# Lo parts from VectorE throughout, and the first weights of the feed-forward layer split ahead of the activations' sums

## The chip, the cores and the metric

The kernel is one program on one NeuronCore of a Trainium2 chip. The metric is the device time of one execution in microseconds (us); lower is better. Engines are named as in the profile: PE (TensorE's matmuls), PEld (its weight loads), DVE (VectorE), ACT (ScalarE), POOL (GpSimd), SP (SyncE, which here issues DMAs).

## The reference, cut to what matters

One layer of a streaming encoder runs over 1088 tokens: 1024 of a prompt and 64 of a sample, with the same weights.

```
xn = rmsnorm(x);  parts = split(xn @ w_in)             # 1024 x 4120
x = x + concat(ya, yb, yc) @ w_out                     # three mixers: RG-LRU, gated linear attention, SSD
g, buf = causal_dwconv(rmsnorm(x) @ w_gate)            # 1024 x 3072, width 3
x = x + (gelu(g) * (rmsnorm(x) @ w_up)) @ w_down
x = x + sigmoid(rmsnorm(x) @ ple_w_gate) * (p @ ple_w_proj)
y = rmsnorm(x)
```

All data are float32, and the outputs are y and the states of the mixers and convolutions.

## The kernel before, in words

**Three matmuls for one.** A float32 product is made from parts in the format F32R: `hi` is the operand rounded to F32R, `lo` is the operand less `hi`, and `w @ x` becomes `wh @ xh + wh @ xl + wl @ xh` (`mm3`, line 156). Each operand that PE reads, a weight or an activation, is therefore split first, by `split` (line 182): ACT writes `hi` (line 184), then one tensor subtraction writes `lo` (line 188). Which engine subtracts is the point of the change. `split` takes an engine as an argument; without one it alternates between VectorE and GpSimd (`alt`, lines 180 to 188). Weights take `wslots["eng"]`, which is GpSimd at first (line 113). At lines 1079 and 1080, before the last third of the output projection, both are set to VectorE. So up to that line all lo parts of weights and every second one of activations are GpSimd's, and after it none are.

**Tokens and units.** Activations lie with features on partitions, in three chunks of 384, 384 and 320 tokens. Weights come in units of 512 KB: `unit_load` (a DMA of SP into `wr`, two buffers) and `unit_split` (into `wh` and `wl`, three buffers in the pool wpool, others at some places). A unit is used for all chunks before the next. While PE does a unit's matmuls, `tick` lets generators ("lanes") emit the small work of the mixers between them.

**Stages.** By the profile's time: norms and first projections (to about 80 us), the rest of the input projection with the RG-LRU, SSD and attention beside it (to 558), the output projection in three thirds (to 721), the per-layer embedding's projection (to 746), the feed-forward layer's gate and up products (to 1263), its down product, the embedding's gate, and the outputs. At the output projection's entry (line 965, `to_parts`) two large activations per chunk are split: `ya`, which goes to the first third at once, and `qk` (into `qh`, `ql`), which goes to the second third.

**The feed-forward entry.** The gate and up products are made by a scheme of seven block products instead of eight (`quad`, line 1169, 256 output columns at a time, `prod` for one product of 24 matmuls). Its operands are sums and differences of blocks. For the activations they are made once (lines 1115 to 1127), in two pieces of 224 and 320 columns: `t1`, `t2`, `t3`, `b22`, `t4`, each split into hi and lo, and from them the matmuls of all 24 quads are fed. For the weights they are made per quad in `quad_weights` (line 1139): two units are loaded, the first is split as it is (`a11`, `a12`), then the sums `s1`, `s2` (tile s12) and `s3`, `s4` (tile s34) are made by VectorE and split as units, and `a22` is split into `dh`, `dl`. The products come in the order a11 (PSUM qa), s2 with t2 (qb), s1 with t1 (qd), a12 (qa), s3 with t3 (qb), s4 with b22 (qd), a22 with t4 (qb), with evacuations by ACT and VectorE between them.

**Where the tiles lie.** Pools are stacks on two sides of the memory. The tiles of t1 and t2 lie exactly over those of the closed pool xnp, t3, b22 and t4 over the closed pools ept and wx (which the embedding's projection reads), and s12, s34, dh and dl in pool w2 behind them. Pool fp, on the other side, with the gate's buffers `fraw`, lies over the closed pool of the residual X0 and X1, of which the sums are made.

**What sets the order.** Each engine runs its instructions in one fixed order. A planner writes it when the kernel is built: by modelled times, it gives an engine the instruction that stands earliest in the program among those that are ready. An instruction whose data are late can so be passed by later ones, and moving lines in the program changes ranks, not places. SP issues its DMAs in such an order too, and each waits there for its buffer.

Of the kernel before, what the change touches and what calls it, by code (L numbers as in the profile page):

```python
# [9 lines left out]
F32 = mybir.dt.float32  # L10
# [5 lines left out]
PSUM = bass.MemoryType.PSUM  # L16
# [15 lines left out]
HF = 544  # L32
# [3 lines left out]
def f32(ap):  # L36
    return ap.bitcast(F32)
# [3 lines left out]
def trunk(ctx: ExitStack, tc: tile.TileContext, I, O):  # L41
    nc = tc.nc
    V, A, G, PE, SY = nc.vector, nc.scalar, nc.gpsimd, nc.tensor, nc.sync

    const = ctx.enter_context(tc.tile_pool(name="const", bufs=1))
    wpool = ctx.enter_context(tc.tile_pool(name="wpool", bufs=3))
# [5 lines left out]
    smps = [smp]  # L52
# [57 lines left out]
            pass  # L110


    wslots = {"pools": [wpool], "n": 0, "eng": G}

    def unit_load(ap):

# [5 lines left out]
    def unit_split(raw):  # L122

        pool = wslots["pools"][wslots["n"] % len(wslots["pools"])]
        wslots["n"] += 1
        hi = pool.tile(list(raw.shape), F32R, tag="wh", name="wh")
        lo = pool.tile(list(raw.shape), F32R, tag="wl", name="wl")
        split(hi, lo, raw, wslots["eng"])
        return hi, lo

    def unit(ap):
# [45 lines left out]
        hl = [xnq.tile([128, 4, TOK], F32R, tag=n, name=n) for n in ("qh", "ql")]  # L177
        return [tuple(t[:, :, t0:t0 + w] for t in hl) for t0, w in CH]

    alt = [V, G]  # L180

    def split(h, l, x, eng=None):

        A.activation(h, x, AF.Copy)  # L184
        if eng is None:
            eng = alt[0]
            alt.reverse()
        eng.tensor_sub(l, x, f32(h))  # L188

    def feat_terms(u, xs, m, nk, k0=0):  # L190
        hi, lo = u
# [110 lines left out]
    smw = sw.tile([128, KD, 40], F32, name="smw")  # L302
    smh = sw.tile([128, KD, 104], F32R, name="smh")
# [4 lines left out]
    finish(*[lane(xblock(b)) for b in range(3)])  # L308
    wq.append(unit_split(wraw))
    V.tensor_scalar(smh[:, :, 40:64], smw[:, :, 0:24], 0.0, None, op0=OP.mult)  # L310
    split(smh[:, :, 0:40], smh[:, :, 64:104], smw, V)

    def proj(u, c):
        ps = mm_tile()
# [103 lines left out]
    for nm in ("lru_w_r", "lru_w_i"):  # L418
        t = lp.tile([128, 4, 128], F32, name=nm + "_bd")
# [233 lines left out]
    ps = sm_tile()  # L653
    PE.matmul(ps[:, :72], tri, dA.rearrange("p b h -> p (b h)"), start=True, stop=True)
    V.tensor_copy(cum.rearrange("p b h -> p (b h)"), ps[:, :72])
    ps = sm_tile()
# [4 lines left out]
    ps = sm_tile()  # L661
# [44 lines left out]
    for i in range(NS):  # L706
        t = gp.tile([128, 2, 2, 128], F32, name=f"Sg{i}")
# [3 lines left out]
    for i in range(2):  # L711
        t = gp.tile([128, 4, 128], F32, name=f"gsT{i}")
# [227 lines left out]
    xst2 = ExitStack()  # L940
# [6 lines left out]
    XK = [xp.tile([128, 4, TOK], F32, name=f"X{i}") for i in range(2)]  # L947
# [87 lines left out]
    def embedding():  # L1035

        pt8 = ept.tile([128, 8, 256], F32, name="pt8")
        pt1 = ept.tile([64, 256], F32, name="pt1")
        src = tokens("p", 0)
        SY.dma_start(pt8, bass.AP(tensor=src.tensor, offset=src.offset, ap=[[256, 128], [128 * 256, 8], [1, 256]]))  # L1040
        SY.dma_start(pt1, tokens("p", 8))
        yield 12
        for b, (c, off, L) in enumerate(BLK):
            pt = pt8[:, b, :] if b < 8 else pt1
            t0 = CH[c][0] + off
            ps = sm_tile()
            for k in range(2):
                PE.transpose(ps[:, k * 128:k * 128 + L], pt[:L, k * 128:(k + 1) * 128], ident[:L, :L])
            yield 1
            split(pTt[0][:, :, t0:t0 + L], pTt[1][:, :, t0:t0 + L],  # L1050
                  ps.rearrange("p (k t) -> p k t", k=4)[:, 0:2, :L], V)
            yield 1

    lefts = []
# [21 lines left out]
            SY.dma_start(xspill[:, m - 1:m + 1, t0:t0 + w], XK[m // 4][:, m % 4 - 1:m % 4 + 1, t0:t0 + w])  # L1076

    emb = lane(embedding())
    alt[:] = [V]
    wslots["eng"] = V  # L1080
    wslots["pools"], wslots["n"] = [wpool, wpool, wpool, wx], 0
    normed = []
    add_proj(WO[1024:1536], ys["c"], 4, lambda c: normed.append(lane(norm_rows(c))), spill)
# [4 lines left out]
    for q in range(2):  # L1088
        u = unit(I["ple_w_proj"][0][:, 512 * q:512 * q + 512])
        for m in range(4):  # L1090
            for c, (t0, w) in enumerate(CH):
                ps = mm_tile()
# [18 lines left out]
    t1, t2 = [half(n, rp1) for n in ("t1", "t2")]  # L1111
    rp2 = rst.enter_context(tc.tile_pool(name="rp2", bufs=1, reuse_waits="tile"))
    t3, b22, t4 = [half(n, rp2) for n in ("t3", "b22", "t4")]
    w2 = rst.enter_context(tc.tile_pool(name="w2", bufs=1, reuse_waits="tile"))
    for a, n in ((0, 224), (224, 320)):
        s = slice(a, a + n)
        x11, x12 = XK[0][:, :, a:a + n], XK[0][:, :, HF + a:HF + a + n]
        x21, x22 = XK[1][:, :, a:a + n], XK[1][:, :, HF + a:HF + a + n]
        V.tensor_sub(x12, x12, x11)
        split(t1[0][:, :, s], t1[1][:, :, s], x12)  # L1120
        V.tensor_sub(x12, x22, x12)
        split(t2[0][:, :, s], t2[1][:, :, s], x12)
        V.tensor_sub(x11, x12, x11)
        V.tensor_sub(x21, x21, x12)
        split(t3[0][:, :, s], t3[1][:, :, s], x11)
        split(b22[0][:, :, s], b22[1][:, :, s], x22)
        split(t4[0][:, :, s], t4[1][:, :, s], x21)
    b11, b21 = [tuple(t[:, 4 * i:4 * i + 4, :] for t in lefts) for i in range(2)]
    xst2.close()

    fst, qpst = ExitStack(), ExitStack()
    fp = fst.enter_context(tc.tile_pool(name="fp", bufs=1, side="right", reuse_waits="tile"))
    qp = qpst.enter_context(tc.tile_pool(name="qp", bufs=1, space=PSUM, reuse_waits="tile"))
    smps[0] = qpst.enter_context(tc.tile_pool(name="smq", bufs=2, space=PSUM, reuse_waits="tile"))
    fouts = fp.tile([128, 96], F32, name="fouts")
    WG, WU, WD = I["ffn_w_gate"][0], I["ffn_w_up"][0], I["ffn_w_down"][0]
    wslots["pools"] = [wpool]

    def quad_weights(ap):

        raw0, raw1 = unit_load(ap[:, 0:128]), unit_load(ap[:, 128:256])
        a11, a12, a21, a22 = raw0[:, 0:4, :], raw0[:, 4:8, :], raw1[:, 0:4, :], raw1[:, 4:8, :]
        al = unit_split(raw0)
        s12 = w2.tile([128, 8, 128], F32, tag="s12", name="s12")
        s1, s2 = s12[:, 0:4, :], s12[:, 4:8, :]
        V.tensor_add(s1, a21, a22)
        V.tensor_sub(s2, s1, a11)
        be = unit_split(s12)
        s34 = w2.tile([128, 8, 128], F32, tag="s34", name="s34")
        s3, s4 = s34[:, 0:4, :], s34[:, 4:8, :]  # L1150
        V.tensor_sub(s3, a11, a21)
        V.tensor_sub(s4, a12, s2)
        ga = unit_split(s34)
        de = tuple(w2.tile([128, 4, 128], F32R, tag=n, name=n) for n in ("dh", "dl"))
        split(de[0], de[1], a22)
        part = lambda u, i: tuple(t[:, 4 * i:4 * i + 4, :] for t in u)
        return {"a11": part(al, 0), "a12": part(al, 1), "s1": part(be, 0), "s2": part(be, 1), "s3": part(ga, 0),
                "s4": part(ga, 1), "a22": de}

    def prod(ps, w, x, new):  # L1160
        for i in range(2):
            n = 0
            for k in range(4):
                for wt, xt in ((w[0], x[0]), (w[0], x[1]), (w[1], x[0])):
                    PE.matmul(ps[:, i, :HI], wt[:, k, :], xt[:, k, HI * i:HI * i + HI], start=new and n == 0,  # L1165
                              stop=n == 11, skip_group_check=True)
                    n += 1

    def quad(ap, take11, o12, o21, o22):

        w = quad_weights(ap)
        A_, B_, D_ = [qp.tile([128, 2, 512], F32, tag=n, name=n) for n in ("qa", "qb", "qd")]
        pa, pb, pd = [t[:, :, :HI] for t in (A_, B_, D_)]
        o12, o21, o22 = [t.rearrange("p (i n) -> p i n", i=2) for t in (o12, o21, o22)]
        prod(A_, w["a11"], b11, True)
        A.activation(o21, pa, AF.Copy)  # L1176
        prod(B_, w["s2"], t2, True)
        V.tensor_add(o12, o21, pb)
        prod(D_, w["s1"], t1, True)
        V.tensor_add(o22, o21, pd)  # L1180
        prod(A_, w["a12"], b21, False)
        take11(pa)
        prod(B_, w["s3"], t3, False)
        V.tensor_add(o22, o22, pb)
        prod(D_, w["s4"], b22, False)
        V.tensor_add(o12, o12, pd)
        prod(B_, w["a22"], t4, False)
        V.tensor_add(o21, o21, pb)
# [21 lines left out]
    Lh, Rh = slice(0, HF), slice(HF, TOK)  # L1210
    for p in range(FF // 256):
        cols = slice(256 * p, 256 * p + 256)
        raws = []
        for i in range(2):
            r = fp.tile([128, 2 + TOK], F32, tag="fraw", name="fraw", bufs=2)
            G.memset(r[:, 0:2], 0.0)
            raws.append(r)
        g0, g1 = [r[:, 2:] for r in raws]

        def to_g11(ps):  # L1220
            A.activation(g0[:, Lh].rearrange("p (i n) -> p i n", i=2), ps, AF.Copy)

        quad(WG[:, cols], to_g11, g0[:, Rh], g1[:, Lh], g1[:, Rh])
        ts = [conv_rows(2 * p + i, raws[i]) for i in range(2)]
        u0 = fp.tile([128, HF], F32, tag="u0", name="u0")
        u1 = fp.tile([128, TOK], F32, tag="u1", name="u1")

        def to_u11(ps):
            t = ts[0][:, Lh].rearrange("p (i n) -> p i n", i=2)
            V.tensor_mul(t, t, ps)  # L1230

        quad(WU[:, cols], to_u11, u0, u1[:, Lh], u1[:, Rh])
        V.tensor_mul(ts[0][:, Rh], ts[0][:, Rh], u0)
        V.tensor_mul(ts[1], ts[1], u1)
        for i in range(2):
            SY.dma_start(hidd[:, 2 * p + i, :], ts[i])

    ps = sm_tile()
# [166 lines left out]
```

## Time and profile before

| | |
|---|---|
| time, median of 3 runs | 1673.28 us (1671.46 to 1674.77) |
| the profiled execution's own time | 1674.28 us |
| its span | 1672.6 us |
| PE busy | 1611.8 us, 96% of the span |
| DVE, ACT, POOL busy | 1064.8, 701.7, 205.7 us |
| mean granted clock of TensorE | 0.982 |

The profile is of one execution. Busy time is the time in which an engine has an instruction under way; for PE, whose matmuls overlap, a window that is fully busy has no gap. The clock is the share of the full 2.4 GHz that was granted: matmuls of a stretch at the lower level of 1.2 GHz take about twice their time. In the lists in order of time a row has its start and length in us, the engine and line, what it writes and reads, its shape, and in brackets how long the engine stood idle before it and which instruction ended that. A line can be a helper's: all lo parts are line 188, all hi parts line 184.

### The profile page before, as it was taken

To read this page: it belongs to the slowest core of one execution; us is meant where nothing else is said; L and a number is where in the kernel's file an instruction comes from. 1 tells how busy PE (TensorE), PEld (TensorE's weight loads), DVE (VectorE), ACT (ScalarE), POOL (GpSimd) and SP (SyncE) were. 2 spreads that over 40 slices of the span, in tenths; PEclk is the share of its full clock that TensorE was granted. 3 is DMA by queue.
4 is the path that set the end of the run, shared out by engine and by line. 5 is a ranking of instruction groups with operands and counts; after the bars stand their busy time and mean duration, and the time that the engine had idled before them with its cause. 6 is when DMAs were issued, how large, how long until landed. Compare 5 with 4: busy or idle time off the path is not lost.

```text
span 1672.6 us, 27037 instructions
## 1 busy us (share of the span) xinstructions
PE 1611.8 (96%) x10990; PEld 1556.1 (93%) x10990; DVE 1064.8 (64%) x1824; ACT 701.7 (42%) x1041; POOL 205.7 (12%) x330
## 2 busy tenths in 40 slices
PE   6999999999999799988999999999999999999997
PEld 6898889878999799988999999999998999999996
DVE  5588883786554853797666766666665544436834
ACT  5578863585722411363333333333333221203526
POOL 3322232221221420000000000000000000000000
PEclk8999999999999999998999999999999999999998
DMA  8332123112652311332222222222228533110223
GB/s 229 89 82 56 48 57 88 39 26 76 174 166 84 98 40 51 114 142 61 78 78 66 88 74 77 75 77 77 77 78 310 175 92 104 55 51 14 79 61 124
DMA packets 169112, 151.80 MB, mean 91 GB/s; under 512 B 11218, under 2 KB 157532, under 8 KB 168988
## 3 DMA queue, kind: packets, MB, share of 16 engines
q1 hardware_dynamic: 159628, 145.62, 28.4%
q10 hardware_dynamic: 9360, 4.46, 0.9%
q8 instruction: 86, 1.41, 0.3%
q14 instruction: 38, 0.31, 0.1%
HBM read 111.26 MB, written 38.79 MB: 90 GB/s over the span
## 4 chain that ended last, share of the span: by engine, by line
PE 61%; DVE 3%; ACT 1%; issue 0%; DVEq 0%; ACTq 0%
PE mm L163 30%; PE qb L1165 13%; PE qd L1165 9%; PE qa L1165 8%; DVE nr_t L218 0%; PE sm L1327 0%; DVE ql L188 0%; ACT yo L1328 0%; DVE X L1062 0%; DVE l L188 0%; DVE yc L986 0%; DVE dl L188 0%; PE sm L216 0%; ACT yo L1338 0%; DVE X L992 0%
## 5 line engine op out<-in xcount | busy, mean ns | idle before, releaser
L163 PE MATMUL mm<-dh,wh 128*128 128x384 f32 (+1 forms) x768 | 252.1, 329 | 2.7 <-ACT wh L184 2.5
L163 PE MATMUL mm<-dl,wh 128*128 128x384 f32 (+1 forms) x768 | 252.0, 328 | 0.8 <-DVE dl L188 0.8
L184 ACT ACTIVATE wh<-wr 128x1024 fp32r<-128x1024 f32 x102 | 107.7, 1058 | 344.7 <-PE mm L163 233.5
L163 PE MATMUL mm<-dh,wl 128*128 128x384 f32 (+1 forms) x768 | 251.4, 328 | 0.0
L163 PE MATMUL mm<-h,wh 128*128 128x384 f32 (+1 forms) x528 | 178.4, 339 | 12.9 <-ACT h L184 8.5
L163 PE MATMUL mm<-l,wh 128*128 128x384 f32 (+1 forms) x528 | 176.9, 335 | 6.2 <-DVE l L188 6.2
L163 PE MATMUL mm<-h,wl 128*128 128x384 f32 (+1 forms) x528 | 179.6, 340 | 0.0
L163 PEld LDWEIGHTS mm<-dh,wh 128*128 128x128 f32 x768 | 145.2, 189 | 3.5 <-ACT wh L184 2.8
L992 DVE TENSOR_TENSOR Xq<-Xq,mm 128x384 f32<-128x384 f32 (+1 forms) x144 | 76.0, 530 | 113.6 <-PE mm L163 113.0
L163 PEld LDWEIGHTS mm<-dl,wh 128*128 128x128 f32 x768 | 145.1, 189 | 1.7 <-DVE dl L188 1.6
L163 PEld LDWEIGHTS mm<-dh,wl 128*128 128x128 f32 x768 | 144.8, 189 | 0.5 <-DVE wl L188 0.3
L163 PE MATMUL mm<-ql,wh 128*128 128x384 f32 (+1 forms) x432 | 143.9, 333 | 0.2 <-POOL ql L188 0.2
L163 PE MATMUL mm<-qh,wh 128*128 128x384 f32 (+1 forms) x432 | 141.9, 328 | 0.0
L163 PE MATMUL mm<-qh,wl 128*128 128x384 f32 (+1 forms) x432 | 141.4, 327 | 0.0
L163 PEld LDWEIGHTS mm<-h,wh 128*128 128x128 f32 x528 | 100.7, 191 | 18.3 <-ACT h L184 9.4
L188 POOL TENSOR_TENSOR wl<-wr,wh 128x1024 fp32r<-128x1024 f32 x40 | 95.8, 2397 | 170.1 <-ACT wh L184 162.6
L184 ACT ACTIVATE wh<-s 128x1024 fp32r<-128x1024 f32 x48 | 51.0, 1061 | 155.2 <-PE qd L1165 55.0
L1165 PE MATMUL qa<-qh,wh 128*128 128x272 f32 x384 | 110.9, 289 | 0.6 <-ACT fraw L1176 0.6
L1165 PE MATMUL qa<-ql,wh 128*128 128x272 f32 x384 | 110.8, 288 | 0.0
L1165 PE MATMUL qa<-qh,wl 128*128 128x272 f32 x384 | 110.4, 288 | 0.0
L163 PEld LDWEIGHTS mm<-l,wh 128*128 128x128 f32 x528 | 101.1, 191 | 9.4 <-DVE l L188 7.0
L163 PEld LDWEIGHTS mm<-h,wl 128*128 128x128 f32 x528 | 101.1, 191 | 2.5 <-issue 0.6
(397 smaller groups left out, 4182.0 us busy)
## 6 DMA issues: line engine op xcount, KB each, us to landing
wr<-in_w_in_dram SPq DMA_DIRECT2D x32, 512.0 KB
hidd<-ft SPq DMA_DIRECT2D x24, 544.0 KB
wr<-in_ffn_w_gate_dram SPq DMA_DIRECT2D x24, 512.0 KB
wr<-in_ffn_w_up_dram SPq DMA_DIRECT2D x24, 512.0 KB
wr<-in_ffn_w_down_dram SPq DMA_DIRECT2D x24, 512.0 KB
st<-hidd SPq DMA_DIRECT2D x12, 768.0 KB
wr<-in_w_out_dram SPq DMA_DIRECT2D x12, 512.0 KB
s_cb<-cumd SPq DMA_DIRECT2D x18, 256.0 KB
```

The costliest lines, as they stand in the source:

```text
L163: PE.matmul(out, w, x, start=(k == 0), stop=(k == n - 1))
L184: A.activation(h, x, AF.Copy)
L188: eng.tensor_sub(l, x, f32(h))
L992: V.tensor_add(xv(c, m), xv(c, m), ps[:, :w])
L1165: PE.matmul(ps[:, i, :HI], wt[:, k, :], xt[:, k, HI * i:HI * i + HI], start=new and n == 0, stop=n == 11, skip_group_check=True)
```

## The change

All lo parts are VectorE's from the beginning: `alt`, the engine argument of `split` and `wslots["eng"]` go, and with them the two lines that switched engines on the way. And `quad_weights` is called for the first 256 columns of the gate ahead of the activations' sums instead of behind them; `quad` takes finished weights. For this the definitions of the weights stand ahead of the sums, and the pools fp, qp and smq are opened after them as before. The other 23 calls of `quad_weights` stand where they stood.

```diff
-    wslots = {"pools": [wpool], "n": 0, "eng": G}
+    wslots = {"pools": [wpool], "n": 0}
...
-        split(hi, lo, raw, wslots["eng"])
+        split(hi, lo, raw)
...
-    alt = [V, G]
-
-    def split(h, l, x, eng=None):
+    def split(h, l, x):
 
         A.activation(h, x, AF.Copy)
-        if eng is None:
-            eng = alt[0]
-            alt.reverse()
-        eng.tensor_sub(l, x, f32(h))
+        V.tensor_sub(l, x, f32(h))
...
-    alt[:] = [V]
-    wslots["eng"] = V
...
-    for a, n in ((0, 224), (224, 320)):
...
-    b11, b21 = [tuple(t[:, 4 * i:4 * i + 4, :] for t in lefts) for i in range(2)]
-    xst2.close()
...
     WG, WU, WD = I["ffn_w_gate"][0], I["ffn_w_up"][0], I["ffn_w_down"][0]
     wslots["pools"] = [wpool]
...
+    first = quad_weights(WG[:, 0:256])
+    for a, n in ((0, 224), (224, 320)):
+        s = slice(a, a + n)
+        x11, x12 = XK[0][:, :, a:a + n], XK[0][:, :, HF + a:HF + a + n]
+        x21, x22 = XK[1][:, :, a:a + n], XK[1][:, :, HF + a:HF + a + n]
+        V.tensor_sub(x12, x12, x11)
+        split(t1[0][:, :, s], t1[1][:, :, s], x12)
+        V.tensor_sub(x12, x22, x12)
+        split(t2[0][:, :, s], t2[1][:, :, s], x12)
+        V.tensor_sub(x11, x12, x11)
+        V.tensor_sub(x21, x21, x12)
+        split(t3[0][:, :, s], t3[1][:, :, s], x11)
+        split(b22[0][:, :, s], b22[1][:, :, s], x22)
+        split(t4[0][:, :, s], t4[1][:, :, s], x21)
+    b11, b21 = [tuple(t[:, 4 * i:4 * i + 4, :] for t in lefts) for i in range(2)]
+    xst2.close()
...
-    def quad(ap, take11, o12, o21, o22):
-
-        w = quad_weights(ap)
+    def quad(w, take11, o12, o21, o22):
+
...
-        quad(WG[:, cols], to_g11, g0[:, Rh], g1[:, Lh], g1[:, Rh])
+        quad(quad_weights(WG[:, cols]) if p else first, to_g11, g0[:, Rh], g1[:, Lh], g1[:, Rh])
...
-        quad(WU[:, cols], to_u11, u0, u1[:, Lh], u1[:, Rh])
+        quad(quad_weights(WU[:, cols]), to_u11, u0, u1[:, Lh], u1[:, Rh])
```

## Rows read from the trace of the kernel before

**Rows 1.** The page's part 1: busy us and share of the span, instructions, of each engine.

```profile
PE 1611.8 (96%) x10990; PEld 1556.1 (93%) x10990; DVE 1064.8 (64%) x1824; ACT 701.7 (42%) x1041; POOL 205.7 (12%) x330
```

**Rows 2.** Windows: us, then busy (x instructions) of PE, PEld, DVE, ACT, POOL; clock, DMA share, GB/s.

```profile
80.00:260.00 180.00, 173.41 (x1092) 159.74 (x1092) 147.56 (x313) 138.47 (x237) 60.20 (x97) 0.98 0.25 64
260.00:420.00 160.00, 157.56 (x1199) 133.72 (x1198) 103.77 (x253) 94.58 (x155) 31.06 (x51) 1.00 0.21 57
...
558.00:594.00 36.00, 26.53 (x134) 24.94 (x133) 34.46 (x31) 11.35 (x14) 15.64 (x5) 0.86 0.25 79
...
746.00:780.00 34.00, 26.52 (x177) 25.58 (x177) 25.39 (x28) 15.21 (x18) 2.84 (x10) 0.80 0.21 63
```

**Rows 3.** PE in order of time, feed-forward's entry: start, us, instruction [idle before <-releaser].

```profile
745.77 0.31 PE L163 MATMUL mm<-pTh,wl 128*128 128x320 f32 x1
...
749.16 0.29 PE L1165 MATMUL qa<-qh,wl 128*128 128x272 f32 x1
...
754.12 0.59 PE L1165 MATMUL qb<-t2h,wh 128*128 128x272 f32 x1 [4.68 <-ACT wh L184]
...
759.17 0.59 PE L1165 MATMUL qb<-t2h,wl 128*128 128x272 f32 x1 [2.17 <-DVE wl L188]
```

**Rows 4.** The chain that ended last: start, us, what; the second quad's first product.

```profile
779.25 3.01 PE qa L1165 x24
```

**Rows 5.** ACT in order of time, feed-forward's entry.

```profile
748.70 0.94 ACT L184 ACTIVATE t4h<-X 128x896 fp32r<-128x896 f32 x1
...
753.02 1.04 ACT L184 ACTIVATE wh<-s 128x1024 fp32r<-128x1024 f32 x1
```

**Rows 6.** DVE in order of time, feed-forward's entry.

```profile
745.48 1.48 DVE L188 TENSOR_TENSOR t2l<-X,t2h 128x1280 fp32r<-128x1280 f32 x1
...
748.28 0.69 DVE L1146 TENSOR_TENSOR s<-wr 128x512 f32<-128x512 f32 x1
...
753.70 1.48 DVE L188 TENSOR_TENSOR t3l<-X,t3h 128x1280 fp32r<-128x1280 f32 x1
...
757.90 1.21 DVE L188 TENSOR_TENSOR wl<-s,wh 128x1024 fp32r<-128x1024 f32 x1
```

**Rows 7.** PE in order of time, output projection's entry.

```profile
574.28 0.63 PE L163 MATMUL mm<-l,wh 128*128 128x320 f32 x1 [5.66 <-DVE l L188]
...
584.22 0.69 PE L163 MATMUL mm<-h,wh 128*128 128x384 f32 x1 [2.29 <-DVE X L992]
```

**Rows 8.** DVE in order of time: operations with two SBUF inputs, three stretches.

```profile
146.21 2.29 DVE L450 SCALAR_TENSOR_TENSOR l_xc<-lraw,cols,l_xc 128x384 f32<-128x384 f32 x1 [0.39 <-ACT l_xc L448]
...
538.95 0.56 DVE L899 SCALAR_TENSOR_TENSOR yc<-yc,gth 128x384 f32<-128x384 f32 x1
...
559.91 2.76 DVE L209 TENSOR_TENSOR nr_t<-nr_t,gy 128x384 f32<-128x384 f32 x1
...
570.05 4.18 DVE L188 TENSOR_TENSOR l<-ya,h 128x1280 fp32r<-128x1280 f32 x1
```

**Rows 9.** POOL in order of time: lo parts beside those.

```profile
145.66 2.42 POOL L188 TENSOR_TENSOR wl<-wr,wh 128x1024 fp32r<-128x1024 f32 x1 [0.57 <-ACT wh L184]
...
562.20 10.68 POOL L188 TENSOR_TENSOR ql<-qk,qh 128x1536 fp32r<-128x1536 f32 x3
```

**Rows 10.** PE in order of time: two waits for DVE.

```profile
150.13 1.16 PE L479 MATMUL sm<-l_xc,lru_w_r_bd 128*128 128x384 f32 x2 [2.14 <-DVE l_xc L450]
...
718.33 0.42 PE L163 MATMUL mm<-h,wh 128*128 128x320 f32 x1 [2.08 <-DVE X L992]
```

**Rows 11.** Line 188 on POOL: ns min/median/max, first and last start us, forms.

```profile
L188 POOL TENSOR_TENSOR wl<-wr,wh x40: 2352/2394/2607, 12.7 to 632.4; 128x1024 fp32r<-128x1024 f32 x40
```

**Rows 12.** PE in order of time: the first projection matmul.

```profile
20.47 1.01 PE L163 MATMUL mm<-h,wh 128*128 128x384 f32 x2 [4.91 <-ACT h L184]
```

**Rows 13.** Waits, whole span: engine line <- releaser: us in total, times, longest us.

```profile
POOL wl L188 <- ACT wh L184: 162.6, 35, 14.1
...
DVE wl L188 <- ACT wh L184: 53.5, 75, 2.8
```

More of the change, by code (lines that the diff above doesn't have):

```diff
@@ L310, in trunk @@
     V.tensor_scalar(smh[:, :, 40:64], smw[:, :, 0:24], 0.0, None, op0=OP.mult)
-    split(smh[:, :, 0:40], smh[:, :, 64:104], smw, V)
+    split(smh[:, :, 0:40], smh[:, :, 64:104], smw)
     def proj(u, c):
@@ L1050, in embedding @@
             split(pTt[0][:, :, t0:t0 + L], pTt[1][:, :, t0:t0 + L],
-                  ps.rearrange("p (k t) -> p k t", k=4)[:, 0:2, :L], V)
+                  ps.rearrange("p (k t) -> p k t", k=4)[:, 0:2, :L])
             yield 1
@@ L1114, in trunk @@
     w2 = rst.enter_context(tc.tile_pool(name="w2", bufs=1, reuse_waits="tile"))
-    for a, n in ((0, 224), (224, 320)):
[L1116 to L1127, printed above, removed]
-    b11, b21 = [tuple(t[:, 4 * i:4 * i + 4, :] for t in lefts) for i in range(2)]
-    xst2.close()
[L1131 to L1135, printed above, removed]
     WG, WU, WD = I["ffn_w_gate"][0], I["ffn_w_up"][0], I["ffn_w_down"][0]
@@ L1158, in quad_weights @@
                 "s4": part(ga, 1), "a22": de}
+    first = quad_weights(WG[:, 0:256])
[14 more added lines that the diff above has]
+    xst2.close()
+    fst, qpst = ExitStack(), ExitStack()
+    fp = fst.enter_context(tc.tile_pool(name="fp", bufs=1, side="right", reuse_waits="tile"))
+    qp = qpst.enter_context(tc.tile_pool(name="qp", bufs=1, space=PSUM, reuse_waits="tile"))
+    smps[0] = qpst.enter_context(tc.tile_pool(name="smq", bufs=2, space=PSUM, reuse_waits="tile"))
+    fouts = fp.tile([128, 96], F32, name="fouts")
     def prod(ps, w, x, new):
```

## The prediction

> **What bounds the kernel now.** I read the busy line of the page first: PE is busy 1611.8 us of a span of 1672.6 [rows 1], so 60.8 us are idle. The reader is to see that no other engine comes near: time can only come from PE's idle time, or from matmuls that run at the lower clock. The windows by stage came next [rows 2]: PE is short by 9.5 us in 558 to 594 (clock 0.86), by 7.5 us in 746 to 780 (clock 0.80) and by 6.6 us in 80 to 260 (clock 0.98). These three stretches hold nearly all that this change can touch. Then I read, for each, PE's order of time and the orders of DVE, ACT and POOL beside it, to see which instruction ended each wait.
>
> *The feed-forward entry.* The first product (qa) ends at 749.3. The second (qb) has to wait 4.68 us for `wh` from ACT, issues two matmuls, does a few of later products, and waits 2.17 us more for `wl` from DVE [rows 3]. The matmul after the wait takes 0.59 us where the last one before it took 0.29: the clock has fallen to its lower level, 1.2 GHz, and the mean over the window is 0.80. The second quad starts at 779.25 [rows 4]. A product of 24 matmuls takes 3.01 us at the full clock [rows 4], so without any wait the six left would end at 749.3 + 6 x 3.01 = 767.4. The entry costs 11.9 us.
>
> Why is `wh` late? ACT makes it at 753.02, behind the six hi parts of t3, b22 and t4, the third of which starts at 748.70 [rows 5]; DVE makes `wl` at 757.90, behind all their lo parts [rows 6]. The order is the program's: the sums and splits stand ahead of the weights. It isn't that the weights could come much sooner: `s12` lies in w2, whose first bytes lie over the end of the closed pool wx (by the tile sizes: t3, b22 and t4 take 52,224 bytes of the 57,344 of ept and wx, then comes `s12`, over the lo part of the projection's second unit). So its first write must wait for the last projection matmul, which starts at 745.77 [rows 3]; the 0.69 us addition stands at 748.28, right behind DVE's older work [rows 6].
>
> *The output projection's entry.* PE waits 5.66 us for a lo part of DVE and later 2.29 us for an accumulation of DVE [rows 7]. DVE is busy 34.46 of these 36 us [rows 2], but not with work: four operations with two SBUF inputs, the first a 2.76 us one at 559.91 and the last one of 4.18 us at 570.05 [rows 8], stand beside POOL's lo parts, 10.68 us for three [rows 9]. The same kind and size takes 0.56 us at 538.95 [rows 8]; a 1280-column lo part takes 1.48 us [rows 6]. Each ends about its own duration after a POOL operation ends (572.88 + 1.4 = 574.2): DVE was held until POOL had finished. The four lost 2.2 + 2.4 + 2.6 + 2.7 = 9.9 us.
>
> **The change, part by part.** Durations are from one execution: 1674.28 us, a span of 1672.6 and 1.7 around it. It lies 1.0 above the median of the runs.
>
> *1. Weights ahead of the sums.* No instruction is added; seven loads, sums and splits change their rank. The two loads are issued as early as before (their buffers are free long ahead), and SP has nothing behind them that waits; the `fp` and quad PSUM pools open later in the text, at the same places. What moves is the order on ACT and DVE after 746. DVE is free at 746.9, behind t2's lo part [rows 6]. s1 and s2 take 0.6 us each from start to start (0.69 with their ends): 748.1. ACT has then three pieces of 0.85 us (dh, t3, b22) behind it and is free at 748.7, where it started t4 before [rows 5]: `wh` is there at 749.7. DVE meanwhile does s3, s4 and the 1.4 us sum that stood ahead of s1 before, to 750.7, then `wl` 1.15 us: 751.9. PE has issued two matmuls of qb by then, 142 of the six products are left, at 3.01 / 24 = 0.125 us: 769.7. That is 9.5 us sooner than 779.25. Bounds: with `wl` straight behind `wh` 10.8, with no wait at all 11.9; if the order stays, nothing. The two waits of together 2.5 us lie near the 2.08 us after which the clock kept its level at 718.33, and near the 2.14 us after which it fell at 150.13 [rows 10]; a fall costs 1.5 us by estimate, a dozen matmuls at twice their time. I take **-9.5**, from 0 to -11.9.
>
> What is late next: t3. Its lo parts stand behind the weights now: 751.9 + 0.6 (dl) + 1.4 and, at the same rate, 1.0 (t3's two parts, [rows 6]) + 1.15 (`wl` of s34) = 756.0, where the last t3 part ended at 755.2 before. It also frees X0, over which the gate's buffer lies, so ACT's evacuation of qa comes at 756.6 and the fourth product can start at 757.2; PE asks for it at 757.7. b22 is done near 759 (asked for at 763.7) and t4 near 762 (at 766.7). These fit, with 0.5 us of slack at the first and 4 us at the others.
>
> *2. The lo parts move to DVE.* 40 weight units at 2.39 us on POOL [rows 11] become 1.15 us each on DVE, 46 us; eight activation parts of 512 columns and one of 256, three of `qk` and one of `yc` add 6 + 5 + 2: 59 us in all, over the first 640 us. Against that stand the times for which POOL held DVE.
>
> At 558 to 594: two units, 2.3, and the three `qk` parts 1.7 + 1.7 + 1.4: 7.1 us more, 9.9 less. From 559.91 to 574.23, the end of the lo part for which PE waited, DVE's 14.3 us become 14.3 - 9.9 + 4.8 + 1.15 = 10.3: the part ends 4.0 us sooner. The second unit may stand in the way of the accumulation for which PE waits 2.29 us: 1.15 back. I take **-3.5**; ends: -8.8 if the `qk` parts, wanted only one projection later, go behind; +2 if both units and all three stand ahead and the release is half of what I read.
>
> At 80 to 260: three times PE waits for `l_xc` of DVE, one of them 2.14 us at 150.13 [rows 10]. Each time the first operation of `l_xc` takes 2.29 us, held by a POOL lo part that began 0.55 us before it [rows 8, 9]. With `wl` ahead of it on DVE it would end at 145.6 + 1.15 + 0.56 = 147.3 and not 148.5, 1.2 us sooner. The other nine of the twelve units there bring 1.15 us each and are hardly paid back. DVE has 32 us idle in the stretch [rows 2]. I take 1 us per wait, **-3**, from -8 (the waits, 5.8, and the clock behind two of them) to the loss of the last rival. From 260 to 420 PE is short by only 2.4 us, and DVE has 56 us idle for 8 us of added units [rows 2]: nothing, plus or minus 2; the ten units up to 558 go the same way.
>
> At the start: PE's first projection matmul waits 4.91 us for the third block's hi part [rows 12], behind DVE's scalings. Ahead of them come now one unit (1.15) and two activation parts (0.6 each), 2.4 in all, less what POOL no longer holds up there. **+1**, from 0 to +2.5.
>
> *The wait that is added.* A lo part waits for ACT's hi part. POOL stood in this wait for 162.6 us, 35 times, harming nobody; where DVE does it, it stands 0.71 us each time (53.5 us, 75 times) [rows 13], with convolutions and accumulations queued behind it. Where ACT is early, as in the forecast, that is idle time that DVE has.
>
> The Trainium skill bears on this in Perfetto Trace Analysis, section Optimizing Scalar/DVE Operations: with a saturated DVE, handing work to GpSimd may pay, though the two share a port and a trade between them might not help. Its first half speaks against this change, its second half is what the held operations show; by the first half alone the output projection's entry would lose, by the time of the first rival.
>
> **The sum.** -9.5 - 3.5 - 3 + 1 = -15.0: 1674.3 becomes 1659.3 for such an execution, and 1658.3 from the median; between the two I say 1659.
>
> **Rivals.**
> - *DVE stays the bound at 558 to 594.* If nothing is given back, 34.46 + 7.1 = 41.6 us of DVE in a stretch of 36: 5.6 us later, not 3.5 sooner, so -5.9: 1668. For it: the 96% load. Against it: the four held operations. Chance 0.08.
> - *The change doesn't do what it says at the feed-forward.* `s12` can't be written before 746, and a planner orders each engine by when an operation is ready: by then t3's parts are ready too and may keep their place. Then only -5.5: 1668.5. Against it: dh, of still lower rank, went ahead of t3 before. Chance 0.08.
> - *The gain is handed back inside the first pair.* If t3 slips by 4 us behind the weights, PE waits at the fourth product, at the lower clock: 1665. Chance 0.12.
> - *DVE gains more*: `qk` parts go behind, the `l_xc` waits vanish with their clock falls: -9.5 - 8 - 7: 1649. Chance 0.10.
> - *Slower: the lo parts clog DVE's queue.* In 80 to 420 DVE holds 19 units, each 1.15 us of work and 0.71 us of wait for ACT ahead of convolutions that PE wants. If all twelve of 80 to 260 come through to PE: 12 x 1.86 = 22.3, with the other terms (-12) +10: 1684. It decides from the seventh that comes through. For it: 147.56 of 180 us busy. Against it: 32 us idle, and weights made a unit ahead. Chance 0.08.
>
> **Chances and range.** Forecast 0.54, within 1653 to 1666. A measurement of this kernel can tell about 0.2%, 3.3 us, from no change. Faster by more: the forecast, the third and fourth rival and half of the first two, 0.84; within it: the other half, 0.08; slower: 0.08. The range, 1650 to 1670, leaves out the slower rival and about half of the 1649 one.
>
> **What would show it.** Right: qb's `wh` on ACT before 750.5 (in time from the end of the projection), the second quad 20 to 22 us after qa's end instead of 30; POOL without lo parts and the 558 to 594 window with no two-input operation of 384 columns on DVE above 0.7 us; `l_xc` waits under 1.5 us. Wrong: ACT or DVE with t3 ahead of `s12`; a wait at the fourth product; PE short in 80 to 420 by more than the 9 us of now.

## The result, and the profile after

The changed kernel takes 1654.82 us (median of 4, 1652.04 to 1658.90) against 1672.37 before: a ratio of 0.9899, with a 95% interval of 0.9870 to 0.9927. Timed a second time beside the experiments below it took 1651.37 us (1650.81 to 1651.61) against 1673.04: 0.9875 (0.9857 to 0.9893). The forecast was 1659, from 1650 to 1670, with a narrower band of 1653 to 1666 for it: the first timing lies in that band, the second 1.6 us under it. Direction and range held. The terms of the sum missed on both sides, and in part made up for one another.

The profiled execution took 1654.01 us. The page's part 1, which answers to [rows 1]:

```profile
PE 1605.0 (97%) x10990; PEld 1551.4 (94%) x10990; DVE 1074.0 (65%) x1877; ACT 699.8 (42%) x1040; POOL 84.1 (5%) x277
```

POOL has lost 122 us, and DVE has gained 9, although 59 us of lo parts moved to it. By that estimate some 50 us of DVE's busy time before were no work of its own.

The windows, as in [rows 2], the third and fourth moved to where the same work now lies:

```profile
80.00:260.00 180.00, 177.46 (x1151) 164.89 (x1150) 151.30 (x330) 139.00 (x240) 34.49 (x86) 1.00 0.27 72
260.00:420.00 160.00, 159.35 (x1204) 135.15 (x1202) 108.92 (x267) 101.08 (x160) 16.40 (x44) 1.00 0.21 55
551.60:587.60 36.00, 33.23 (x183) 31.60 (x182) 31.45 (x42) 11.07 (x13) 0.00 (x0) 0.95 0.29 93
731.60:765.60 34.00, 30.27 (x224) 29.55 (x224) 31.04 (x37) 18.97 (x22) 3.56 (x13) 0.95 0.27 79
```

PE's idle time fell in every one, and the clock rose in the first, third and fourth. Following the same matmul through both traces gives each term (the forecast's stretches end a little elsewhere):

| up to | before | after | forecast of this stretch | measured |
|---|---|---|---|---|
| first projection matmul | 20.47 | 24.24 | +1 | +3.8 |
| first matmul of the values' projection | 214.24 | 210.42 | -3 | -7.6 |
| statistics at the output projection's entry | 557.88 | 551.49 | 0 | -2.6 |
| embedding's projection | 721.46 | 706.94 | -3.5 | -8.1 |
| first feed-forward product | 746.15 | 731.74 | 0 | +0.1 |
| second quad (chain of waits) | 779.25 | 758.89 | -9.5 | -6.0 |
| end of the span | 1672.6 | 1652.3 | 0 | +0.1 |

A second profile of the changed kernel, from its second timing, gives each of these within 0.7 us, except the last, which is -1.5 there.

The feed-forward entry in PE's order of time (a row has its start and length, and in brackets the wait and what ended it), answering to [rows 3]; under it two pieces of the chain of waits, answering to [rows 4]:

```profile
735.50 0.39 PE L1160 MATMUL qb<-t2h,wh 128*128 128x272 f32 x1 [0.47 <-ACT wh L182]
...
736.76 0.39 PE L1160 MATMUL qb<-t2h,wl 128*128 128x272 f32 x1 [0.49 <-DVE wl L183]
...
745.24 0.59 PE L1160 MATMUL qa<-qh,wh 128*128 128x272 f32 x1 [2.69 <-ACT fraw L1170]
```

```profile
757.89 1.00 PE qb L1160 x8
758.89 1.13 PE qa L1160 x9
```

The two waits that the reordering was to shorten fell from 4.68 and 2.17 us to 0.47 and 0.49. In their place stands one of 2.69 us at the fourth product, for ACT's evacuation of qa. The matmul behind it takes 0.59 us: the clock is at its lower level again.

The output projection's entry on PE, answering to [rows 7], and DVE beside it, answering to [rows 8]:

```profile
561.21 0.78 PE L211 MATMUL sm<-nr_t,ones 128*128 128x320 f32 x2 [0.67 <-DVE nr_t L204]
...
564.09 0.61 PE L163 MATMUL mm<-h,wh 128*128 128x320 f32 x1 [2.10 <-DVE X L987]
```

```profile
552.04 0.55 DVE L204 TENSOR_TENSOR nr_t<-nr_t,gy 128x384 f32<-128x384 f32 x1
552.51 1.22 DVE L183 TENSOR_TENSOR wl<-wr,wh 128x1024 fp32r<-128x1024 f32 x1
553.64 3.42 DVE L183 TENSOR_TENSOR ql<-qk,qh 128x1536 fp32r<-128x1536 f32 x2
...
557.38 1.48 DVE L183 TENSOR_TENSOR ql<-qk,qh 128x1280 fp32r<-128x1280 f32 x1
...
559.18 1.48 DVE L183 TENSOR_TENSOR l<-ya,h 128x1280 fp32r<-128x1280 f32 x1
560.59 0.48 DVE L204 TENSOR_TENSOR nr_t<-nr_t,gy 128x320 f32<-128x320 f32 x1
...
563.45 0.49 DVE L987 TENSOR_TENSOR X<-X,mm 128x384 f32<-128x384 f32 x1
```

The 0.55 us operation took 2.76 us before and the lo part of ya 4.18. Three ql parts and a unit now stand ahead of that lo part, and PE doesn't wait for it. The 320-column nr_t operation and the accumulations into X come behind it; before, that nr_t operation and two accumulations stood ahead (at 567.03, 562.59 and 566.35).

The waits for l_xc, answering to [rows 10]:

```profile
124.05 0.91 PE L474 MATMUL sm<-l_xc,lru_w_r_bd 128*128 128x384 f32 x2 [1.40 <-DVE l_xc L445]
...
152.87 0.91 PE L474 MATMUL sm<-l_xc,lru_w_r_bd 128*128 128x384 f32 x2 [0.27 <-DVE l_xc L445]
...
181.50 0.91 PE L474 MATMUL sm<-l_xc,lru_w_r_bd 128*128 128x384 f32 x2 [0.82 <-DVE l_xc L445]
```

### The profile page after: what moved, and what is told of

Same layout as the page of the kernel before. It is cut to its first block, busy times and chain, and to the rows that moved or that the text cites. A ratio compares the mean times of both kernels' runs of the same rounds, so it can differ in the third digit from the quotient of the medians.

```text
span 1652.3 us, 26989 instructions
## 1 busy us (share of the span) xinstructions
PE 1605.0 (97%) x10990; PEld 1551.4 (94%) x10990; DVE 1074.0 (65%) x1877; ACT 699.8 (42%) x1040; POOL 84.1 (5%) x277
## 4 chain that ended last, share of the span: by engine, by line
PE 87%; DVE 6%; ACT 3%; DMA 2%; issue 1%; SPq 0%; ACTq 0%; POOL 0%; DVEq 0%; POOLq 0%
PE mm L163 49%; PE qb L1160 13%; PE qd L1160 9%; PE qa L1160 9%; DMA xsp<-x 1%; PE po L794 1%; DMA wr<-in_w_in_dram 1%; PE sm L579 1%; PE sm L800 1%; PE po L787 1%; PE sm L581 0%; PE sm L575 0%; DVE l_xc L445 0%; PE sm L474 0%; DVE xs L445 0%
## 5 line engine op out<-in xcount | busy, mean ns | idle before, releaser
L183 DVE TENSOR_TENSOR wl<-wr,wh 128x1024 fp32r<-128x1024 f32 x102 | 124.8, 1225 | 63.3 <-ACT wh L182 63.1
```

The source lines that it names most:

```text
L183: V.tensor_sub(l, x, f32(h))
```

## The experiments

Theory: the two parts act at different places; GpSimd's subtractions hold VectorE's operations with two SBUF inputs, and the first part's gain is the end of that; the second part's gain is cut by the evacuation of qa. Rivals: the gain is one of VectorE's order or load; the fourth product's wait is a late VectorE's. Times below are medians, and ratios stand against the kernel before on the same chip, which took 1672.5, 1673.0 and 1672.1 us in the three sets of runs. Each set had a chip of its own, and the changed kernel was timed again only in the second; where a run of another set is compared with it, the ratios count.

**Each part alone.** The first without the second:

```diff
-    first = quad_weights(WG[:, 0:256])
...
-        quad(quad_weights(WG[:, cols]) if p else first, ...)
+        quad(quad_weights(WG[:, cols]), ...)
```

> Only the first part of the change: all lo parts are VectorE's, the first pair's weights stay behind the sums. Theory (the two parts are separate, and the first one brings what the changed kernel had gained by the start of the feed-forward layer, 14.4 us): the first feed-forward product starts near 731.7, the second quad 29 to 31 us behind the end of qa as before, time 1659 to 1661. Rival (the terms as I sized them, -5.5 in all): 1667 to 1669.

1658.01 us, ratio 0.9908 (0.9896 to 0.9921): 14.5 sooner, 1 us better than the theory had it. The first product starts at 730.31, the second quad 29.3 us behind the end of qa, and the wait for `wh` is back:

```profile
738.28 0.58 PE L1159 MATMUL qb<-t2h,wh 128*128 128x272 f32 x1 [4.70 <-ACT wh L182]
```

The second without the first (`alt`, `eng` and both switches as before, `first` ahead of the sums):

> Only the second part: the first pair's weights ahead of the sums, the lo parts on their engines of before. Theory: nothing moves before 746; the second quad starts 24 us behind the end of qa and not 30, with a wait of 2 to 3 us at the fourth product, time 1667 to 1669 for an execution of 1674. Rival (the fourth product's wait comes from VectorE being late by work of the first part): no such wait, second quad 20.5 us behind, 1664 to 1665.

1666.65 us, 0.9954 (0.9939 to 0.9970): 5.9 sooner, which lies between theory and rival. The trace decides: the fourth product waits the same 2.69 us with the lo parts on their old engines, so the rival falls. The second quad starts 22.4 us behind the end of qa and not 24, as the clock stayed up behind that wait:

```profile
760.88 0.39 PE L1167 MATMUL qa<-qh,wh 128*128 128x272 f32 x1 [2.69 <-ACT fraw L1177]
```

The two add up to 20.4; the whole change brought 17.6 and 21.7 in its two timings.

**What the fourth product waits for.** From the first product's start to the third quad's, two quads without a wait take 14 x 3.01 = 42.1 us. Before it was 54.0, in the changed kernel 48.0 and 48.2, with the first part alone 53.7. With t3 ahead:

```diff
     for a, n in ((0, 224), (224, 320)):
...
         split(t3[0][:, :, s], t3[1][:, :, s], x11)
+    for a, n in ((0, 224), (224, 320)):
...
         split(b22[0][:, :, s], b22[1][:, :, s], x22)
         split(t4[0][:, :, s], t4[1][:, :, s], x21)
```

> The changed kernel with the sums of both column pieces up to t3 ahead of the splits of b22 and t4, so that X0 is read for the last time two VectorE operations (2.0 us) sooner. Theory A (X0's last read holds the gate's buffer, and so the evacuation of qa): the wait of 2.69 us at the fourth product falls to 0.7 and the clock stays up, 3 to 4 us sooner than the changed kernel, 1651. Rival B (ScalarE's own queue of hi parts holds that evacuation, at best till 743.4 where it was 744.58): the wait falls by 1.2 us only, 1 to 1.5 us sooner, 1653.5.

1650.72 us, 0.9866 (0.9852 to 0.9880). In the changed kernel DVE's last t3 part and ACT's rows ahead of the evacuation are these:

```profile
738.76 1.09 DVE L183 TENSOR_TENSOR b22l<-X,b22h 128x896 fp32r<-128x896 f32 x1
739.76 1.09 DVE L183 TENSOR_TENSOR t4l<-X,t4h 128x896 fp32r<-128x896 f32 x1
740.76 1.48 DVE L1142 TENSOR_TENSOR X<-X,X 128x1280 f32<-128x1280 f32 x1
742.16 1.48 DVE L183 TENSOR_TENSOR t3l<-X,t3h 128x1280 fp32r<-128x1280 f32 x1
```

```profile
742.46 1.06 ACT L182 ACTIVATE wh<-wr 128x1024 fp32r<-128x1024 f32 x1 [1.21 <-PE qd L1160]
743.42 1.25 ACT L182 ACTIVATE t4h<-X 128x1280 fp32r<-128x1280 f32 x1
744.58 0.60 ACT L1170 ACTIVATE fraw<-qa 128x544 f32<-128x544 f32 x1
```

X0 is free at 743.64, and ACT is in t4's hi part until 744.58. With t3 ahead, PE's two waits and ACT's evacuation:

```profile
740.41 0.39 PE L1163 MATMUL qa<-qh,wh 128*128 128x272 f32 x1 [1.58 <-ACT fraw L1173]
...
744.56 0.39 PE L1163 MATMUL qb<-t3h,wh 128*128 128x272 f32 x1 [0.86 <-DVE fraw L1175]
```

```profile
737.84 1.08 DVE L183 TENSOR_TENSOR b22l<-X,b22h 128x896 fp32r<-128x896 f32 x1
```

```profile
737.43 1.25 ACT L182 ACTIVATE t4h<-X 128x1280 fp32r<-128x1280 f32 x1
738.79 1.06 ACT L182 ACTIVATE wh<-wr 128x1024 fp32r<-128x1024 f32 x1
739.75 0.60 ACT L1173 ACTIVATE fraw<-qa 128x544 f32<-128x544 f32 x1
```

X0 is free at 737.9, when DVE starts b22, but ACT evacuates at 739.75, behind its own hi parts. The wait fell by 1.11 us, as rival B had it, and a new one of 0.86 came behind it. (The total is nearer theory A, but it can't tell the two: the changed kernel's own ratios are 0.9899 and 0.9875.) The two-quad stretch is 46.7 us, the 1.3 less being nearly all clock: with the second part alone, where the 2.69 us wait stayed and the clock didn't fall, it is 46.7 too. So for this order both X0's last read and ACT's queue hold the evacuation. The other way is to take X0 out of it:

```diff
+    fp2 = fst.enter_context(tc.tile_pool(name="fp2", bufs=1, side="right", reuse_waits="tile"))
     fouts = fp.tile([128, 96], F32, name="fouts")
+    fp.tile([128, 2624], F32, name="pad")
...
-            r = fp.tile([128, 2 + TOK], F32, tag="fraw", name="fraw", bufs=2)
+            r = (fp, fp2)[i].tile([128, 2 + TOK], F32, tag="fraw", name="fraw")
```

> The changed kernel with the gate's buffer that takes the evacuation of qa laid behind X0 and X1 in memory, not over X0; the rest of the buffers lie over X0 and X1 in another order. Theory A (the overlap with X0 causes the fourth product's wait): ScalarE evacuates qa near 741.5, no wait of over 0.5 us at the fourth product, its first 13 matmuls at full clock: 2.7 + 1.6 = 4.3 us sooner than the changed kernel, 1650.5. Rival B (ScalarE's queue is late anyway): less than 1.5 us sooner, 1653.5. Rival C: the buffers that lie over X0 and X1 now make another wait, no sooner than the changed kernel.

1650.51 us, 0.9864 (0.9851 to 0.9877). ACT now has the evacuation between b22 and t4, and the wait at the fourth product is gone; two short ones follow:

```profile
742.79 0.60 ACT L1172 ACTIVATE fraw<-qa 128x544 f32<-128x544 f32 x1
```

```profile
747.91 0.39 PE L1162 MATMUL qa<-qh,wh 128*128 128x272 f32 x1 [0.71 <-ACT fraw L1217]
...
748.79 0.39 PE L1162 MATMUL qd<-b22h,wh 128*128 128x272 f32 x1 [0.49 <-DVE fraw L1176]
```

The two-quad stretch is 45.5 us, 2.5 less than in the changed kernel: theory A in kind, but 2.5 and not 4.3, since evacuations further on are late in turn (two waits, 1.2 us together and 1.6 us from matmul to matmul). The total agrees no better than that: 0.9 us under one timing of the changed kernel and 4.3 under the other, neither taken beside this run.

**GpSimd's hold, by itself.** VectorE's program stays, and GpSimd makes each weight's lo part of the RG-LRU stage again, for nobody:

```diff
         split(hi, lo, raw)
+        for pool in twice:                  # lp, the RG-LRU stage's pool, while it is open
+            again = pool.tile([128, 1024], F32, tag="again", name="again")
+            G.tensor_sub(again.rearrange("p (k n) -> p k n", k=raw.shape[1]), raw, f32(hi))
         return hi, lo
```

> The changed kernel, with the lo part of each weight unit of the RG-LRU stage (9 units, some 80 to 215 us) made a second time by GpSimd into a scratch that nobody reads. VectorE's instructions are the changed kernel's. Theory (a two-input operation of GpSimd holds VectorE's two-input operations): VectorE's operations of l_xc and its lo parts beside the copies last 2 us and more, the waits for l_xc come back as 1.5 to 2.2 us three times, 4 to 7 us later than the changed kernel, 1656 to 1661. Rival (VectorE's own load and order make these waits): nothing changes, within 1.5 us of the changed kernel.

1659.01 us, 0.9928 (0.9909 to 0.9948), where the changed kernel beside it took 1651.37: 7.6 later. Of these, 6.2 us have come together by the first matmul of the values' projection (215.77 against 209.53). (The trace shows eight copies, not nine, and one lo part of VectorE, near 85, stands some operations later; behind it VectorE's order is that of the changed kernel.) The window 80 to 260, first of the changed kernel timed beside it, then of this one:

```profile
80.00:260.00 180.00, 178.40 (x1164) 165.65 (x1164) 151.73 (x331) 138.93 (x241) 34.38 (x86) 1.00 0.27 71
```

```profile
80.00:260.00 180.00, 172.89 (x1102) 159.61 (x1101) 161.65 (x327) 137.42 (x236) 53.01 (x92) 0.99 0.25 65
```

DVE is busy 9.9 us longer with no operation more; six of the copies, 18.2 us, start in this window. Around 150, POOL, DVE and the matmul that waits:

```profile
148.27 6.58 POOL L132 TENSOR_TENSOR again<-wr,wh 128x1024 f32<-128x1024 f32 x2 [0.58 <-ACT wh L186]
```

```profile
149.88 2.77 DVE L450 SCALAR_TENSOR_TENSOR l_xc<-lraw,cols,l_xc 128x384 f32<-128x384 f32 x1
152.57 3.37 DVE L187 TENSOR_TENSOR wl<-wr,wh 128x1024 fp32r<-128x1024 f32 x1
```

```profile
157.58 1.65 PE L479 MATMUL sm<-l_xc,lru_w_r_bd 128*128 128x384 f32 x2 [4.57 <-DVE l_xc L450]
```

In the changed kernel that l_xc operation takes 0.61 us and the unit 1.21. POOL's pair ends at 154.85, and the unit's lo part 1.09 us later. The rival, load and order, is out. The waits came back otherwise than I had written, 2.51 and 4.57 us and none at the third place, where no copy stood. The Trainium skill has this as a rule, in SBUF — State Buffer, section SBUF: two separate sides: of a VectorE operation with two SBUF inputs and a GpSimd operation that reads SBUF, the one that starts first holds the shared ports for its whole length and the other stands still. That rule names one more kind of VectorE operation, those in a two-port performance mode, and the start shows two operations that aren't of the two-input kind, one that kept its time and one that didn't (below).

**The output projection's entry, by itself.** Before, with only the switch moved ahead:

```diff
+    alt[:] = [V]
+    wslots["eng"] = V
     gate(2576, gate_c, between)
...
     emb = lane(embedding())
-    alt[:] = [V]
-    wslots["eng"] = V
```

> The kernel before with one thing else: both switches to VectorE stand ahead of the last gate projection, so that the lo parts from there on, qk's among them, are VectorE's; all earlier ones stay, and the feed-forward order is that of before. Theory (GpSimd's lo parts hold VectorE at the output projection's entry, 8 us from 558 to 721 by itself): PE's waits at the entry are one of 2.1 us and one of 0.7 where they were 1.5, 5.7 and 2.3, time 1664 to 1665.5. Rival (that stretch was quicker only because VectorE came into it less late after an earlier start): 1669 or more.

1665.33 us, 0.9961 (0.9945 to 0.9976): 7.7 sooner, as theory had it, with the waits of the changed kernel:

```profile
572.25 0.78 PE L216 MATMUL sm<-nr_t,ones 128*128 128x320 f32 x2 [0.68 <-DVE nr_t L209]
...
575.12 0.38 PE L163 MATMUL mm<-h,wh 128*128 128x320 f32 x1 [2.10 <-DVE X L994]
```

And the reverse, only qk's three lo parts on GpSimd:

```diff
-        split(h, l, x)
+        split(h, l, x, G if key == "b" else V)
```

> The changed kernel with only the three lo parts of qk, at the output projection's entry, back on GpSimd. VectorE has three operations less in that stretch (4.8 us). Theory (while GpSimd subtracts, VectorE's two-input operations stand still): VectorE's operations beside them last 2 to 4 us each, PE waits 4 us or more for a lo part or an accumulation near 558 to 580, 3 to 6 us later than the changed kernel, 1655 to 1659. Rival (VectorE's load decides there, 34 of 36 us): VectorE is through 4.8 us sooner, the changed kernel's waits of 0.7 and 2.1 us shrink, 1648 to 1651.

1655.71 us, 0.9900 (0.9886 to 0.9914). This total by itself shows no loss: the changed kernel's ratios are 0.9899 and 0.9875, and it was not timed beside this run (its second timing is 4.3 us lower). The trace does. The three parts take POOL 10.8 us, the two-input operation and the lo part beside them 3.14 and 4.17, while an accumulation that reads PSUM (`mm`) keeps its 0.54, and PE waits as in [rows 7]:

```profile
552.32 10.82 POOL L183 TENSOR_TENSOR ql<-qk,qh 128x1536 fp32r<-128x1536 f32 x3 [78.16 <-ACT qh L182]
```

```profile
556.58 0.54 DVE L987 TENSOR_TENSOR X<-X,mm 128x384 f32<-128x384 f32 x1
557.25 3.14 DVE L204 TENSOR_TENSOR nr_t<-nr_t,gy 128x320 f32<-128x320 f32 x1
560.32 4.17 DVE L183 TENSOR_TENSOR l<-ya,h 128x1280 fp32r<-128x1280 f32 x1
```

```profile
564.54 0.64 PE L163 MATMUL mm<-l,wh 128*128 128x320 f32 x1 [5.68 <-DVE l L183]
```

From the 384-column nr_t operation to the end of that lo part DVE takes 13.3 us, in the changed kernel 8.6, and PE takes 159.2 us from the statistics to the embedding's projection, in the changed kernel's two profiles 155.5 and 154.9. Handing three operations to an idle engine made the busier one slower. Of the sentence that the forecast drew from the Trainium skill (Perfetto Trace Analysis, Optimizing Scalar/DVE Operations), it is the second half, that such a trade might not help, that this trace bears out.

**The start.** The lo parts up to the third token block as before, the rest on VectorE:

```diff
     finish(*[lane(xblock(b)) for b in range(3)])
+    alt[:] = [V]
+    wslots["eng"] = V
```

> The changed kernel, with the lo parts up to and including the third token block on the engines of before (the first weight unit on GpSimd, the activations in turn), the rest on VectorE. Theory (VectorE's lo parts ahead of the third block's scalings cost the 3 us at the start): the first projection matmul at 20.5 to 21.0, not 23.3 to 24.2, and the shift lasts: 3 us sooner than the changed kernel, 1650 to 1651.5. Rival (given back: ScalarE and the DMA of the tokens set the pace of the later blocks): first matmul at 20.5 to 21 but the third chunk of tokens ready as late as now, within 1 us of the changed kernel.

1647.87 us, 0.9857 (0.9838 to 0.9876): 3.5 sooner than the changed kernel beside it, and the first projection matmul at 19.80, where that one has it at 23.57. Here GpSimd costs little, and the profile shows why. POOL's unit and DVE beside it:

```profile
12.04 2.36 POOL L188 TENSOR_TENSOR wl<-wr,wh 128x1024 fp32r<-128x1024 f32 x1 [9.81 <-ACT wh L184]
```

```profile
12.75 0.59 DVE L272 SCALAR_TENSOR_TENSOR xg<-sm,cols,rb 128x128 f32<-128x128 f32 x2
13.26 0.86 DVE L272 SCALAR_TENSOR_TENSOR xg<-mm,cols,rb 128x128 f32<-128x128 f32 x3
14.04 0.91 DVE L188 TENSOR_TENSOR l<-xg,h 128x512 fp32r<-128x512 f32 x1
```

The scalings read PSUM (`sm`, `mm`) and take 0.33 to 0.34 us each, as they do in the changed kernel with no GpSimd operation beside them; the lo part, with two SBUF inputs, is stretched from 0.69 to 0.91. It isn't two inputs alone, though. Somewhat later an operation with a single input in SBUF is held as well:

```profile
20.69 2.18 POOL L188 TENSOR_TENSOR ql<-xg,qh 128x512 fp32r<-128x512 f32 x1 [0.64 <-ACT qh L184]
```

```profile
21.65 1.33 DVE L312 TENSOR_SCALAR smh<-smw 128x192 fp32r<-128x192 f32 x1
```

In the changed kernel it takes 0.25. Whether it is of the rule's second kind no run here shows.

**Together.** The start's engines and the clear buffer; then t3 ahead as well:

> The changed kernel with two of the edits together: the first lo parts on the engines of before, and the gate's buffer clear of X0. Theory (they act at places far apart and add up, -3.5 and -2.5): 1645 to 1646.5. Rival (one eats the other's gain): not under 1647.5.

> As the kernel with the two edits, and the sums up to t3 ahead of b22 and t4 as well. Theory (both last edits act on the same wait, which the clear buffer has taken away already): within 1 us of the kernel with two edits. Rival (t3's earlier lo part takes away the 0.7 and 0.5 us that are left behind the fourth product): 1 to 2 us sooner, 1644.

1646.15 us, 0.9844 (0.9830 to 0.9859), and 1645.70, 0.9842 (0.9826 to 0.9858). The two-quad stretch is 45.5 us in both: the edits for start and buffer add up, and t3's place brings nothing once the buffer is clear. Both ratios lie below the changed kernel's two, 0.9899 and 0.9875, though it was not timed beside them.

## Why the prediction was right, and where it was wrong

The direction was right for the reasons given: GpSimd held VectorE, and the first weights stood behind the sums. That the total came within the range owes something to luck. For the profiled execution -15.0 was forecast and -20.3 measured: three stretches brought 11.8 us more than forecast, the others 6.5 less.

*Feed-forward entry, -9.5, measured -6.0.* `wh` came as worked out, and `wl` 0.8 us sooner. The step that failed is t3's: its lo parts were to end at 756.0, "with 0.5 us of slack at the first". That sum left out two lo parts that DVE does before t3's second piece, b22 and t4 of the first piece, 1.0 us each from start to start; they stood there before as well (at 751.70 and 752.70). On the new clock 756.0 is 741.6; the part ended at 743.64, 2.0 later, and ACT's t4 came on top. The price was a wait of 2.69 us and a fall of the clock: the 24 matmuls of qa took 4.5 us from start to start instead of 3.0. A wait at the fourth product stood among the signs of being wrong. It is the third rival, handed back inside the first pair, at a little over half of the size I gave it, and at the buffer that I had named as the next thing late, not at t3 itself.

*Output projection's entry, -3.5, measured -8.1 (7.7 by itself).* The mechanism was right, the term mis-sized. From nr_t's start to the end of the lo part for which PE waits, I had DVE's 14.3 us become 10.3; they became 8.6 (552.04 to 560.66). The three ql parts and a unit stand ahead, as I had put them, but two accumulations and the second nr_t operation, some 1.3 us without a hold, went behind, and for that the sum had no term. They also began 1.5 us sooner, counted from the statistics. That covers the whole 5.66 us wait, and the clock over these 36 us rose from 0.86 to 0.95.

*l_xc, -3, measured -7.6 (by the values' projection).* The mechanism was right, the term mis-sized. I counted 1 us for each wait and nothing for the clock. The three waits fell by 3.3 us (5.8 to 2.5), PE's busy time in the window rose by 4.1, and the clock from 0.98 to 1.00. I had this as the end of the range and as the fourth rival; where a wait lets the clock fall, the two go together.

*The start, +1, measured +3.8.* The mistake was "less what POOL no longer holds up there": next to nothing was held, since the scalings read PSUM. And it isn't one unit and two activation parts that came ahead of the scalings for the third block's first hi part but one unit and three parts, 3.0 us, with 0.5 us in which DVE waits for a hi part. The rest is of this execution: ACT's hi part of the first unit starts at 12.14 where it started at 11.57 before. The changed kernel's second profile has the matmul at 23.57, which is +3.1.

*260 to 558, nothing plus or minus 2, measured -2.6 (from 214 on).* PE's shortfall in 260 to 420 went from 2.4 to 0.7 us.

*The other rivals.* The slower one found no support: from 80 to 420 PE waits for no lo part. Over the first 640 us DVE was given 59 us of work and, by the same estimate, relieved of some 50 us of holds. The first rival, DVE as the bound at the output projection's entry, falls with the three parts handed back to GpSimd. The second, an order that doesn't change, falls with ACT's and DVE's order at the feed-forward entry, where `wh` and `wl` stand ahead of t3's parts.

*What stays open.* Five profiles of kernels with the same order on PE up to the feed-forward layer reach its first product between 728.0 and 733.4, with clocks of 0.89 to 1.00 in 700 to 732. And behind the same 2.69 us wait the clock fell in three profiles (the changed kernel's two, the one with the start's engines) and stayed in three (the second part alone, qk on GpSimd, the lo parts made twice). What decides that was not found. So a difference of less than some 3 us in the total of two profiles shows nothing by itself, and the two timings of the changed kernel lie 3.4 us apart as well.

## What to carry to other kernels

Before work goes to GpSimd, or back from it, look at what VectorE does beside it: here operations with two SBUF inputs stood still until GpSimd had finished (2.76 us instead of 0.55), and a tensor_scalar with one SBUF input did too (1.33 instead of 0.25), while those that read PSUM kept their time. An engine's busy share doesn't show this; the same kind and size of operation at two very different durations does. When a stall at a shared entry is removed, list every instruction ahead of the next one due, on each engine, and the buffers that open only when these are through.

## What the runs showed of the hardware

GpSimd's hold cost VectorE half to three quarters of GpSimd's own time. Before, four lo parts of 13.2 us at the output projection's entry lost it 9.9 us; the three of 10.8 us in the kernel with qk on GpSimd lost it 7.0; and the eight copies of 24.9 us lost it 13.1 over its first 400 operations, in a stretch where it has other work between. The hold may go both ways: GpSimd's copies took 3.11 us on average where its lo parts took 2.39 before. That VectorE's two-input operations hold GpSimd in turn is the likely reason, and was not tried by itself.
